# First norm's chains in turn, C's transposes in banks of their own, and four last stores instead of eight

## The chip, the core and the metric

One core of a Trainium2 chip runs the whole program. It has five engines, each with an in-order stream of instructions: TensorE (PE: matmuls and transposes, with PEld for the loading of weights), VectorE (DVE), ScalarE (ACT), GpSimd (POOL) and SyncE (SP), which here only issues DMA transfers. ScalarE issues some too. Work is handed from one to another by semaphores. The metric is the device time of one execution in microseconds (us), the median over several runs.

## What is computed

Two layers on x (256 tokens, width 1024), each of the form h + Mixer(RMSNorm(h)): first native sparse attention (16 heads in 4 groups: compressed, selected and window branches), then an S5 diagonal state-space mixer, and a final RMSNorm. The parts that the change touches:

```python
def _rmsnorm(x, g):
    y = x * lax.rsqrt(jnp.mean(x * x, axis=-1, keepdims=True) + EPS) * g

# attention: q, k, v, gates, z = split(h @ w_in); compressed, selected, window; @ w_out

# S5, parameters only (no token enters here):
    dt = jnp.exp(log_dt)[:, None]
    lre = jnp.minimum(lambda_re, -1e-4)
    mag = jnp.exp(lre * dt)
    ab_re, ab_im = mag * jnp.cos(lim * dt), mag * jnp.sin(lim * dt)
    den = lre * lre + lim * lim
    coef = (ab - 1) / lambda                     # complex
    bb_re = coef_re[..., None] * b_re - coef_im[..., None] * b_im
    bb_im = coef_re[..., None] * b_im + coef_im[..., None] * b_re
# S5, tokens: a linear scan with ab, y = Re(C x) + d * u, gelu, glu, * silu(z), @ w_out

    return _rmsnorm(h, final_norm)
```

## The kernel before

The 256 tokens lie as two tiles (NQ = 2, index j) of 128 partitions. The **first norm** sums the squares of each tile (ScalarE, L336), makes 1/sqrt with a few tiny VectorE operations (`rsqrt_steps`, tiles rs_v, rs_i, rs_t, rs_y), spreads the result along a row with a diagonal matrix and a matmul (`row_bcast`, L312 and L313; the row is copied to rrow), and multiplies the transposed x by it and by the weight: eight products xn of 128x256 (L350), one for each 128 channels. Its VectorE, GpSimd and ScalarE instructions stand in the order of the code (`manual_schedule`). Elsewhere a scheduler fixes, when the program is built, the order of each engine's instructions; on the chip each engine keeps that order.

Then the **first layer's projections** run on TensorE, each 16 matmuls of 128x256 (32 in the trace, where one fp32 matmul is two records): v0, v1 (L280), k0, k1 (L267), the gates gt, and more. Each k projection is followed by ScalarE's kh (its rounded copy, L791) and VectorE's kl (the rest, L795), which empties its PSUM bank. The small transpose cm (L875) turns a tile `rows` of parameters, which SyncE loads (L355 to L362).

Beside these projections, a generator `s5_gen` prepares the **second layer's parameters**. `chain_gen` computes dt and the powers' first factors on VectorE; their rows `nat` are transposed on TensorE into bank bg (L493), and VectorE copies them to pT (L494, all parameters with one column for each state). VectorE builds the powers pw from pT, real part pw[:, 0] and imaginary part pw[:, 1], doubling their number three times (L377, tile c is scratch), and copies eight of them to a tile named h in the trace (L532). GpSimd forms B's products from them (b1c, h, ep: six products of 128x1024, L383). C's rows are transposed in two rounds of four (q = 0, 1; L544), and ScalarE copies each round out of PSUM as c1c and c2c (L546, L548). GpSimd multiplies c1c by the real powers (ep<-c1c,pw, L383). The first four of these need the first round only, but the fourth overwrites a place from which the second round reads.

A bank of PSUM is one of eight. `bg_bank` gives the one bank of the generator, `bank(tag, 1)` one of a phase; tu and ob are tags that the attention's units use later.

At the **end**, the last projection's second tile (j = 1) is taken in three pieces (0:512, 512:768, 768:1024 columns), each added to h, squared and summed; the root follows, and `finish(1)` scales the columns and stores them. The stores are 32 rows each.

Of the kernel before, what the change touches and what calls it, by code (L numbers as in the profile page):

```python
# [8 lines left out]
F32 = mybir.dt.float32  # L9
# [3 lines left out]
ALU = mybir.AluOpType  # L13
# [33 lines left out]
def kernel(  # L47
# [52 lines left out]
    def bank(tag="b1", bufs=None):  # L100
        return phase["pool"].tile([P, 512], F32, tag=tag, name=tag, bufs=bufs or phase["bufs"])
# [181 lines left out]
    def rsqrt_steps(ss, out_, part=None):  # L283


        v = smp.tile([P, 1], F32, tag="rs_v", name="rs_v")
        V.tensor_scalar(v, ss, 1.0 / D, EPS if part is None else part, op0=ALU.mult, op1=ALU.add)
        yield
        yi = smp.tile([P, 1], I32, tag="rs_i", name="rs_i")
        V.tensor_scalar(yi, v.bitcast(I32), -0.5, float(0x5F3759DF), op0=ALU.mult, op1=ALU.add)  # L290
        yield
        y, c = yi.bitcast(F32), 1.0
        t = smp.tile([P, 1], F32, tag="rs_t", name="rs_t")
        z = smp.tile([P, 1], F32, tag="rs_y", name="rs_y")
# [31 lines left out]
    xn = actp.tile([P, KT, S], F32, tag="actT", name="xn")
    sqs = xn.rearrange("p (j k) s -> p j (k s)", j=NQ)
    bts = [bank().rearrange("p (k s) -> p k s", k=2) for _ in range(KT // 2)]
    rb, gb0 = bank(), bank()
    rrow = const.tile([P, S], F32, name="rrow")  # L330
    E_ = mybir.EngineType
    with tc.manual_schedule(engines={E_.DVE, E_.Pool, E_.Activation}):
        sums, ys = [], [[], []]
        for j in range(NQ):
            sums.append(smp.tile([P, 1], F32, tag="ss", name="ss"))
            A.activation(sqs[:, j], xin[:, j], AF.Square, accum_out=sums[j])  # L336
            for k in range(KT):
                T.transpose(bts[k // 2][:, k % 2, j * P:(j + 1) * P], xin[:, j, k * P:(k + 1) * P], ident)
        rq = [rsqrt_steps(sums[j], ys[j]) for j in range(NQ)]
        for _ in range(6):  # L340
            next(rq[0])
        for r in (rq[1], rq[0]) * 12:
            next(r, None)
        for j in range(NQ):
            row_bcast(*ys[j], rb[:, j * P:(j + 1) * P], sqs[:, j, 0:P])
        T.transpose(gb0[:, :KT], nrow, ident[:KT, :KT])
        V.tensor_copy(g0c, gb0[:, :KT])
        V.tensor_copy(rrow, rb[:, :S])
        for k in range(KT):
            V.scalar_tensor_tensor(xn[:, k], bts[k // 2][:, k % 2], g0c[:, k:k + 1], rrow,  # L350
                                   op0=ALU.mult, op1=ALU.mult)
        s5_loads()

    rows = const.tile([56, P], F32, name="rows")
    nc.sync.dma_start(rows[8:24], pe_k.rearrange("(k l) d -> k (l d)", l=2))  # L355
    nc.sync.dma_start(rows[24:40], pe_v.rearrange("(k l) d -> k (l d)", l=2))
    nc.sync.dma_start(rows[0:8], n1.rearrange("(k p) -> k p", p=P))
    nc.sync.dma_start(rows[40:48], d_skip.rearrange("(k g) c -> k (g c)", k=8))
    d4 = d_skip.rearrange("(k j u) c -> u k j c", k=8, j=4)
    r4 = rows[48:56].rearrange("k (j u c) -> k u j c", j=4, u=2)  # L360
    for u in range(2):
        nc.sync.dma_start(r4[:, u], d4[1 - u])  # L362
    colsT = const.tile([P, 56], F32, name="colsT")


    bbT.insert(0, (0, actp.tile([P, NB0, P], F32, tag="actT", name="bbT0")))
# [27 lines left out]
    def chain_gen():  # L394
# [84 lines left out]
        A.activation(nat2[:, 4:7, 1], nat[:, 4:7], AF.Copy)  # L479
        yield  # L480

    sh_ld = {}

    def s5_gen():
# [54 lines left out]
        yield  # L539

        for q in range(2):
            bt2 = bg_bank()
            for t in range(4):
                T.transpose(bt2[:, t * P:(t + 1) * P], cnat[:, 4 * q + t].rearrange("p r q -> p (r q)"), ident)  # L544
            gs = slice(32 * q, 32 * q + 32)
            A.activation(c1c[:, gs].rearrange("p g c -> p (g c)"), bt2, AF.Copy, scale=nsg)  # L546
            for hf in range(2):
                A.activation(c2c[64 * hf:64 * hf + 64, gs].rearrange("p g c -> p (g c)"),  # L548
                             bt2[64 - 64 * hf:128 - 64 * hf], AF.Copy, scale=-1.0)
            yield  # L550
# [89 lines left out]
            yield  # L640

    with tc.high_priority(-CHOFF):
        for _ in chain_gen():
            pass
    bg = s5_gen()

# [17 lines left out]
    PL.iota(cdist, pattern=[[P, NQ], [-16, NB]], base=0, channel_multiplier=1,  # L664
            allow_small_or_imprecise_dtypes=True)
    PL.tensor_scalar(cdist, cdist, -15.5, None, op0=ALU.add)
    cbias = atp.tile([P, NQ, 16, NB], F32, name="cbias")
    slopes = atp.tile([P, 16], F32, name="slopes")
    for h in range(16):
        PL.memset(slopes[:, h:h + 1], -_slope(h))  # L670
# [777 lines left out]
    def piece(i, src):  # L1448

        j, c0, c1 = pieces[i]  # L1450
        V.tensor_tensor(h1s[j][:, c0:c1], src, h1s[j][:, c0:c1], op=ALU.add)
        A.activation(ho[j][:, c0:c1], h1s[j][:, c0:c1], AF.Square, accum_out=sq[:, i:i + 1])
        if i == 4:
            return
        PL.tensor_tensor(hg[j][:, c0:c1], h1s[j][:, c0:c1], gf[:, c0:c1], op=ALU.mult)

    def finish(j, i):
        y, c = rsqrt_mean(sq[:, i:i + 1], vp[j])
        assert c == RSQRT_C
        if j == 0:  # L1460
            A.activation(ho[0], hg[0], AF.Copy, scale=y)
            for l_ in range(4):
                nc.sync.dma_start(o3[0, l_], ho[0][32 * l_:32 * l_ + 32])
            return
        A.activation(ho[1][:, 0:512], hg[1][:, 0:512], AF.Copy, scale=y)
        V.scalar_tensor_tensor(ho[1][:, 768:D], h1s[1][:, 768:D], y, gf[:, 768:D], op0=ALU.mult, op1=ALU.mult)
        V.tensor_scalar(ho[1][:, 512:768], hg[1][:, 512:768], y, None, op0=ALU.mult)
        for l_ in range(4):
            nc.sync.dma_start(o3[1, l_, :, 0:512], ho[1][32 * l_:32 * l_ + 32, 0:512])
        for l_ in range(4):  # L1470
            (nc.scalar, nc.sync)[l_ % 2].dma_start(o3[1, l_, :, 512:D], ho[1][32 * l_:32 * l_ + 32, 512:D])
# [68 lines left out]
```

## Time and profile before

| | |
|---|---|
| median of three runs | 413.06 us (411.81 to 414.19) |
| the profiled execution | 414.05 us |
| its span, first to last instruction | 412.3 us |
| busy: PE, PEld | 354.2 us (86%), 293.0 us (71%) |
| busy: DVE, ACT, POOL | 227.9 us (55%), 178.4 us (43%), 269.3 us (65%) |
| DMA | 52.03 MB, mean 126 GB/s |
| mean granted clock of TensorE | 0.933 |

A row of the timeline gives the start, the length, the engine, the line of the code, the operation, its output and input tiles, how many instructions are grouped (x4), and in square brackets how long the engine was idle before it and what ended that.

### The profile page before, as it was taken

The page shows a single profiled execution, that of the slowest core. Times are in us where ns is not written, and L with a number is a line of the kernel's source. Part 1 is how long each engine was busy: PE and PEld are TensorE (multiplying, and loading weights), DVE is VectorE, ACT ScalarE, POOL GpSimd, SP SyncE. Part 2 cuts the span into 40 slices and gives each one's busy share as a digit, 9 for nine tenths or more (in the row PEclk, how much of TensorE's full clock was granted, in tenths as well). Part 3 has the DMA queues.
Part 4 walks back from the last instruction along what each step waited for, and adds up shares of the span by engine and source line. Part 5 has one row for each costly group of instructions (what it writes and reads, how often), then busy time and mean ns, then how long its engine had stood idle before and what let it go on. Part 6 is the DMA issues. An engine that isn't in the chain of part 4 may idle for free.

```text
span 412.3 us, 6834 instructions
## 1 busy us (share of the span) xinstructions
PE 354.2 (86%) x2505; PEld 293.0 (71%) x2505; DVE 227.9 (55%) x582; ACT 178.4 (43%) x397; POOL 269.3 (65%) x281
## 2 busy tenths in 40 slices
PE   3899599999999998968998879994858599999990
PEld 3688468865888787644766657783847599999890
DVE  4969904433355243524555498563999944264243
ACT  3212420145366467566784454342513335444432
POOL 7009459989987789999544489321872476665760
PEclk9699979999999999985999999998696899999996
DMA  8964315558633315411311335996741215655403
GB/s 256 158 172 114 110 53 153 152 190 244 181 103 99 106 57 178 126 52 51 103 36 58 113 103 99 172 87 180 251 156 54 71 34 158 199 163 200 152 2 102
DMA packets 59970, 52.03 MB, mean 126 GB/s; under 512 B 21928, under 2 KB 52704, under 8 KB 59872
## 3 DMA queue, kind: packets, MB, share of 16 engines
q1 hardware_dynamic: 49536, 50.41, 43.9%
q10 hardware_dynamic: 10400, 1.18, 2.2%
q8 instruction: 20, 0.33, 0.4%
q14 instruction: 14, 0.11, 0.1%
HBM read 48.17 MB, written 1.05 MB: 119 GB/s over the span
## 4 chain that ended last, share of the span: by engine, by line
PE 57%; DVE 16%; SPq 6%; POOL 6%; DMA 5%; issue 5%; ACT 3%; DVEq 0%; ACTq 0%; POOLq 0%
PE b L267 16%; SPq L1181 5%; PE b L280 4%; PE b L224 4%; PE b L225 4%; PE b L226 4%; PE ob L986 3%; PE tu L973 2%; PE b L246 2%; PE b L244 2%; PE b L245 2%; DVE pw L377 2%; POOL wl L209 2%; PE cm L745 2%; DVE bbT L1357 2%
## 5 line engine op out<-in xcount | busy, mean ns | idle before, releaser
L209 POOL TENSOR_TENSOR wl<-raw,wh 128x1024 fp32r<-128x1024 f32 x30 | 74.3, 2480 | 48.3 <-ACT wh L207 48.1
L267 PE MATMUL b<-xn,raw 128*128 128x256 f32 (+1 forms) x400 | 94.9, 390 | 4.7 <-DVE kl L795 3.4
L267 PEld LDWEIGHTS b<-xn,raw 128*128 128x128 f32 (+1 forms) x400 | 74.1, 190 | 18.6 <-issue 4.6
L207 ACT ACTIVATE wh<-raw 128x1024 fp32r<-128x1024 f32 x48 | 50.8, 1058 | 67.0 <-PE b L225 20.7
L209 DVE TENSOR_TENSOR wl<-raw,wh 128x1024 fp32r<-128x1024 f32 x18 | 26.3, 1462 | 26.3 <-ACT wh L207 26.3
L959 ACT ACTIVATE pt<-pt,nm 128x128 f32<-128x128 f32 (+1 forms) x64 | 28.3, 444 | 24.8 <-DVE nm L955 24.7
L225 PE MATMUL b<-yl,wh 128*128 128x256 f32 x128 | 36.1, 283 | 0.0
L224 PE MATMUL b<-yh,wh 128*128 128x256 f32 x128 | 36.1, 284 | 0.0
L226 PE MATMUL b<-yh,wl 128*128 128x256 f32 x128 | 36.0, 283 | 0.0
L975 DVE COPY pT<-tu 128x512 f32<-128x512 f32 x24 | 16.6, 691 | 25.4 <-PE tu L973 24.7
L968 ACT ACTIVATE pt<-pt,su 128x128 f32<-128x128 f32 (+1 forms) x64 | 24.6, 443 | 11.6 <-DVE su L966 11.5
L224 PE MATMUL b<-xp,wh 128*128 128x256 f32 x64 | 20.2, 317 | 5.7 <-ACT wh L207 5.7
L224 PEld LDWEIGHTS b<-yh,wh 128*128 128x128 f32 x128 | 24.5, 192 | 0.2 <-issue 0.2
L225 PEld LDWEIGHTS b<-yl,wh 128*128 128x128 f32 x128 | 24.6, 192 | 0.0
L226 PEld LDWEIGHTS b<-yh,wl 128*128 128x128 f32 x128 | 24.5, 192 | 0.0
L383 POOL TENSOR_TENSOR ep<-c1c,pw 128x1024 f32<-128x1024 f32 x8 | 16.0, 2022 | 10.3 <-ACT c1c L546 5.3
L955 DVE CUSTOM_DVE_ANT_0 pt<-su,b 128x128 f32<-128x128 f32 (+1 forms) x64 | 19.4, 351 | 4.7 <-PE su L943 4.7
L226 PE MATMUL b<-xp,wl 128*128 128x256 f32 x64 | 20.1, 316 | 1.6 <-POOL wl L209 1.6
L383 POOL TENSOR_TENSOR bbn<-bbn,bbt 128x512 f32<-128x512 f32 x16 | 20.4, 1274 | 0.6
L383 POOL TENSOR_TENSOR bbn<-b1c,h 128x512 f32<-128x512 f32 x16 | 17.8, 1111 | 4.6 <-PE bg L604 4.4
L986 PE MATMUL ob<-pT,vsw 128*64 128x128 f32 x192 | 17.4, 297 | 3.4 <-DVE pT L975 3.4
L225 PE MATMUL b<-xp,wh 128*128 128x256 f32 x64 | 19.8, 311 | 0.0
(319 smaller groups left out, 874.1 us busy)
## 6 DMA issues: line engine op xcount, KB each, us to landing
raw<-in_l_w_in_dram SPq DMA_DIRECT2D x44, 512.0 KB, 4.0
raw<-in_l_w_out_dram SPq DMA_DIRECT2D x16, 512.0 KB, 3.9
raw<-in_l_w_glu_dram SPq DMA_DIRECT2D x16, 512.0 KB, 3.6
raw<-in_l_cmp_k_w_dram SPq DMA_DIRECT2D x4, 512.0 KB, 3.9
raw<-in_l_cmp_v_w_dram SPq DMA_DIRECT2D x4, 512.0 KB, 3.9
xin<-in_x_dram SPq DMA_DIRECT2D x2, 512.0 KB
h<-in_x_dram SPq DMA_DIRECT2D x8, 128.0 KB, 3.3
tm<-kt__2197 SPq DMA_DIRECT2D x4, 128.0 KB
```

What stands on the lines that cost most here:

```text
L207: A.activation(hi, raw, AF.Copy)
L209: lo_eng[-1].tensor_tensor(lo, raw, hi.bitcast(F32), op=ALU.subtract)
L224: T.matmul(dst, a, xh[:, k], start=(k == 0 and e == 0), stop=False)
L225: T.matmul(dst, a, xl[:, k], start=False, stop=False)
L226: T.matmul(dst, b, xh[:, k], start=False, stop=(k == KT - 1 and e == len(dsts) - 1))
L267: T.matmul(dst, w[:, i, e * m:(e + 1) * m], xn[:, k], start=(k == 0 and e == 0), stop=(k == KT - 1 and e == len(dsts) - 1))
L383: PL.tensor_tensor(o, a, b_, op=op)
L955: V.tensor_tensor_reduce(o.rearrange("p t k -> p (t k)"), sb[:, i * w + br * nk:i * w + (br + 1) * nk], self.b8[hf][:, S - nk:S], -0.125, ...
L959: A.activation(o, o, AF.Exp, scale=-1.0, bias=self.nm[:, j, hf, br:br + 1], accum_out=self.su[:, j, hf, br:br + 1])
L968: A.activation(o, o, AF.Copy, scale=r)
L986: T.matmul(self.ob[64 * hf:64 * hf + 64, j * P:(j + 1) * P], vsw[:, kt, br, 64 * g:64 * g + 64], p_, start=first, stop=last, tile_position ...
L1181: nc.sync.dma_start(tm[16 * s_:16 * s_ + 16, 16 * j:16 * j + 16].rearrange("p q l c -> p q (l c)")[:, :, 16 * l_:P], kt_[32 * j:32 * j + 1 ...
```

## The change

The first norm's second sum of squares goes from ScalarE to VectorE, and the two chains of tiny operations run strictly in turn. The diagonals are written into the tile cbias, so that tile is opened earlier. The first three pieces of `chain_gen` are issued behind the norm's products, no longer among them. C's two rounds of transposes take the banks tu and ob instead of bg. At the end, GpSimd no longer multiplies the piece 512:768, one VectorE operation covers 512:1024, and tile j = 1 is stored by four transfers of 32x1024, one from SyncE and three from ScalarE, instead of eight of 32x512.

```diff
+    att = tc.tile_pool(name="att", bufs=1, reuse_waits="tile")
+    atp = att.__enter__()
+    cbias = atp.tile([P, NQ, 16, NB], F32, name="cbias")
...
     with tc.manual_schedule(engines={E_.DVE, E_.Pool, E_.Activation}):
-        sums, ys = [], [[], []]
-        for j in range(NQ):
-            sums.append(smp.tile([P, 1], F32, tag="ss", name="ss"))
-            A.activation(sqs[:, j], xin[:, j], AF.Square, accum_out=sums[j])
+        sums, ys = smp.tile([P, NQ], F32, name="ss0"), [[], []]
+        A.activation(sqs[:, 0], xin[:, 0], AF.Square, accum_out=sums[:, 0:1])
+        V.tensor_tensor_reduce(sqs[:, 1], xin[:, 1], xin[:, 1], 1.0, 0.0, ALU.mult, ALU.add, sums[:, 1:2])
+        for j in range(NQ):
             for k in range(KT):
                 T.transpose(bts[k // 2][:, k % 2, j * P:(j + 1) * P], xin[:, j, k * P:(k + 1) * P], ident)
-        rq = [rsqrt_steps(sums[j], ys[j]) for j in range(NQ)]
-        for _ in range(6):
-            next(rq[0])
-        for r in (rq[1], rq[0]) * 12:
+        rq = [rsqrt_steps(sums[:, j:j + 1], ys[j]) for j in range(NQ)]
+        T.transpose(gb0[:, :KT], nrow, ident[:KT, :KT])
+        for r in rq * 12:
             next(r, None)
         for j in range(NQ):
-            row_bcast(*ys[j], rb[:, j * P:(j + 1) * P], sqs[:, j, 0:P])
-        T.transpose(gb0[:, :KT], nrow, ident[:KT, :KT])
+            row_bcast(*ys[j], rb[:, j * P:(j + 1) * P], cbias[:, j, 0:8].rearrange("p h n -> p (h n)"))
...
         s5_loads()
+        chain = chain_gen()
+        for _ in range(3):
+            next(chain)
...
         for q in range(2):
-            bt2 = bg_bank()
+            bt2 = bank(("tu", "ob")[q], 1)
             for t in range(4):
                 T.transpose(bt2[:, t * P:(t + 1) * P], cnat[:, 4 * q + t].rearrange("p r q -> p (r q)"), ident)
...
     with tc.high_priority(-CHOFF):
-        for _ in chain_gen():
+        for _ in chain:
             pass
...
-        if i == 4:
+        if i >= 3:
             return
...
-        V.scalar_tensor_tensor(ho[1][:, 768:D], h1s[1][:, 768:D], y, gf[:, 768:D], op0=ALU.mult, op1=ALU.mult)
-        V.tensor_scalar(ho[1][:, 512:768], hg[1][:, 512:768], y, None, op0=ALU.mult)
+        V.scalar_tensor_tensor(ho[1][:, 512:D], h1s[1][:, 512:D], y, gf[:, 512:D], op0=ALU.mult, op1=ALU.mult)
         for l_ in range(4):
-            nc.sync.dma_start(o3[1, l_, :, 0:512], ho[1][32 * l_:32 * l_ + 32, 0:512])
-        for l_ in range(4):
-            (nc.scalar, nc.sync)[l_ % 2].dma_start(o3[1, l_, :, 512:D], ho[1][32 * l_:32 * l_ + 32, 512:D])
+            (nc.sync if l_ == 1 else nc.scalar).dma_start(o3[1, l_], ho[1][32 * l_:32 * l_ + 32])
```

What stands on TensorE from cm to the gates before (one row of 128x256 x16 is one projection: v1 and k0, k1 by their b tiles; gt is the one of 48x256; nat are the powers' rows, ep C's rows):

```order
L875 MATMUL cm<-ident,rows 128x56
L280 MATMUL b_402<-raw,xn 128x256 x14
L493 MATMUL bg<-ident,nat_106 128x64 x4
L280 MATMUL b_402<-raw,xn 128x256 x2
L267 MATMUL b_433<-xn,raw 128x256 x9
L493 MATMUL bg<-ident,nat_106 128x64 x3
L267 MATMUL b_433<-xn,raw 128x256 x7
L267 MATMUL b_485<-xn,raw 128x256 x16
L544 MATMUL bg<-ident,ep 128x128 x4
L267 MATMUL b_530<-xn,raw 48x256 x8
L267 MATMUL b_558<-xn,raw 128x256 x4
L544 MATMUL bg<-ident,ep 128x128 x4
```

And after the change, the same place on TensorE (v1 is b_401, k0 b_432, k1 b_484, gt b_529):

```order
L878 MATMUL cm<-ident,rows 128x56
L285 MATMUL b_401<-raw,xn 128x256 x16
L272 MATMUL b_432<-xn,raw 128x256 x4
L499 MATMUL bg<-ident,nat_106 128x64 x4
L272 MATMUL b_432<-xn,raw 128x256 x11
L499 MATMUL bg<-ident,nat_106 128x64 x3
L272 MATMUL b_432<-xn,raw 128x256
L272 MATMUL b_484<-xn,raw 128x256 x16
L550 MATMUL tu<-ident,ep 128x128 x4
L550 MATMUL ob<-ident,ep 128x128
L272 MATMUL b_529<-xn,raw 48x256 x8
L550 MATMUL ob<-ident,ep 128x128 x3
```

The powers' first transposes moved behind the last two matmuls of v1 and the first four of k0, the second ones behind fifteen of k0 instead of nine. C's first round stands where it stood, in bank tu; one transpose of the second round moved ahead of the gates and the other three right behind them.

On SyncE, the stores at the end of the program before (tm is the tile of the results):

```order
L1463 DMA out_dram<-tm 32x1024 x4
L1469 DMA out_dram<-tm 32x512 x4
L1471 DMA out_dram<-tm 32x512 x2
```

After, on SyncE, the same stores:

```order
L1466 DMA out_dram<-tm 32x1024 x4
L1471 DMA out_dram<-tm 32x1024
```

And on ScalarE after, whose last row read 32x512 x2 before:

```order
L1464 ACTIVATE tm<-tm,rs_y 128x1024
L1468 ACTIVATE tm<-tm,rs_y 128x512
L1471 DMA out_dram<-tm 32x1024 x3
```

Of the second tile's eight stores four are left; three of the four moved behind ScalarE's product of the columns 0:512, and SyncE issues one.

## Rows read from the trace of the kernel before

**Rows 1.** Chain that ended last on the page: share of the span by engine.

```profile
PE 57%; DVE 16%; SPq 6%; POOL 6%; DMA 5%; issue 5%; ACT 3%; DVEq 0%; ACTq 0%; POOLq 0%
```

**Rows 2.** Stretches: length, busy us of PE, PEld, DVE, ACT, POOL; PE clock, DMA share, GB/s.

```profile
46.40:56.40 10.00, 6.48 (x18) 3.31 (x19) 5.68 (x20) 3.23 (x6) 5.97 (x3) 0.66 0.19 52
...
80.00:150.00 70.00, 68.99 (x428) 54.07 (x428) 28.32 (x103) 34.21 (x108) 59.09 (x62) 1.00 0.50 145
150.00:198.00 48.00, 41.49 (x251) 30.49 (x250) 18.31 (x68) 31.63 (x87) 46.30 (x56) 0.86 0.32 104
```

**Rows 3.** TensorE's timeline: start us, us, line, operation, tiles, idle time before and its releaser.

```profile
13.11 10.00 PE L280 MATMUL b<-raw,xn 128*128 128x256 f32 x32 [1.81 <-issue]
23.05 0.27 PE L875 MATMUL cm<-ident,rows 56*128 56x56 f32 x1
23.24 6.31 PE L280 MATMUL b<-raw,xn 128*128 128x256 f32 x28
29.48 0.46 PE L493 MATMUL bg<-ident,nat 64*128 64x64 f32 x4
...
46.49 0.66 PE L544 MATMUL bg<-ident,ep 128*128 128x128 f32 x4 [1.16 <-DVE pT L494]
50.58 8.45 PE L267 MATMUL b<-xn,raw 128*48 128x256 f32 x24 [3.43 <-DVE kl L795]
```

**Rows 4.** VectorE's timeline, 30 to 52 us.

```profile
30.61 1.93 DVE L372 TENSOR_SCALAR cis<-pT,sgn 128x64 f32<-128x64 f32 x1
...
36.49 2.37 DVE L532 COPY h<-pw 128x128 f32<-128x128 f32 x1
...
41.11 2.26 DVE L377 TENSOR_TENSOR pw<-pw,c 128x64 f32<-128x64 f32 x1
...
46.35 0.42 DVE L377 TENSOR_TENSOR pw<-pw,c 128x256 f32<-128x256 f32 x1
...
48.05 0.63 DVE L532 COPY h<-pw 128x128 f32<-128x128 f32 x4
48.60 3.48 DVE L795 TENSOR_TENSOR kl<-b,kh 64x256 fp32r<-64x256 f32 x8
```

**Rows 5.** GpSimd's timeline, 30 to 55 us.

```profile
30.48 2.00 POOL L383 TENSOR_TENSOR b1c<-ep,pT 128x1024 f32<-128x1024 f32 x1 [22.10 <-DVE pT L494]
...
40.88 2.42 POOL L383 TENSOR_TENSOR h<-h,ep 128x1024 f32<-128x1024 f32 x1
48.62 5.97 POOL L383 TENSOR_TENSOR ep<-c1c,pw 128x1024 f32<-128x1024 f32 x3 [5.33 <-ACT c1c L546]
```

**Rows 6.** ScalarE's timeline, first norm and C.

```profile
5.75 1.06 ACT L336 ACTIVATE xn<-xin 128x1024 f32<-128x1024 f32 x1 [0.31 <-DMA xin<-in_x_dram]
...
47.80 0.69 ACT L546 ACTIVATE c1c<-bg,nsg 128x512 f32<-128x512 f32 x1
```

**Rows 7.** VectorE's timeline, first norm.

```profile
7.94 0.14 DVE L287 TENSOR_SCALAR rs_v<-ss 128x1 f32<-128x1 f32 x1
...
9.62 0.16 DVE L299 SCALAR_TENSOR_TENSOR rs_y<-rs_t,rs_y 128x1 f32<-128x1 f32 x1
...
11.68 0.53 DVE L419 RECIPROCAL den<-den 64x64 f32<-64x64 f32 x1
...
12.15 3.21 DVE L350 SCALAR_TENSOR_TENSOR xn<-b,g0c,rrow 128x256 f32<-128x256 f32 x8
```

**Rows 8.** SyncE's queue, the last loads of the rows.

```profile
18.41 1.56 SPq L362 DMA_DIRECT2D rows<-in_l_d_dram  x2
```

**Rows 9.** SyncE's queue, last stores.

```profile
409.15 0.84 SPq L1471 DMA_DIRECT2D out_dram<-tm  x2
```

**Rows 10.** ScalarE's queue, last stores.

```profile
406.29 0.85 ACTq L1471 DMA_DIRECT2D out_dram<-tm  x2
```

**Rows 11.** VectorE's timeline, last product.

```profile
405.50 0.48 DVE L1466 SCALAR_TENSOR_TENSOR tm<-h,rs_y,gf 128x256 f32<-128x256 f32 x1
```

**Rows 12.** TensorE's timeline, the taps of the second layer.

```profile
241.56 1.08 PE L634 MATMUL bg<-ep,b1c 128*32 128x128 f32 x32 [2.56 <-ACT kt__2197 L638]
```

More of the change, by code (lines that the diff above doesn't have):

```diff
@@ L324 @@
         prefetch(w_in0, 4 * c_, 4, FIRST[1], 256)
[L326 to L332, printed above, removed]
-        sums, ys = [], [[], []]
-        for j in range(NQ):
-            sums.append(smp.tile([P, 1], F32, tag="ss", name="ss"))
-            A.activation(sqs[:, j], xin[:, j], AF.Square, accum_out=sums[j])
-            for k in range(KT):
-                T.transpose(bts[k // 2][:, k % 2, j * P:(j + 1) * P], xin[:, j, k * P:(k + 1) * P], ident)
-        rq = [rsqrt_steps(sums[j], ys[j]) for j in range(NQ)]
-        for _ in range(6):
-            next(rq[0])
-        for r in (rq[1], rq[0]) * 12:
-            next(r, None)
-        for j in range(NQ):
-            row_bcast(*ys[j], rb[:, j * P:(j + 1) * P], sqs[:, j, 0:P])
-        T.transpose(gb0[:, :KT], nrow, ident[:KT, :KT])
[L347 to L366, printed above, removed]
     MAGIC = 12582912.0
@@ L480, in chain_gen @@
         yield
+    xn = actp.tile([P, KT, S], F32, tag="actT", name="xn")
+    sqs = xn.rearrange("p (j k) s -> p j (k s)", j=NQ)
+    bts = [bank().rearrange("p (k s) -> p k s", k=2) for _ in range(KT // 2)]
+    rb, gb0 = bank(), bank()
+    rrow = const.tile([P, S], F32, name="rrow")
+    E_ = mybir.EngineType
+    with tc.manual_schedule(engines={E_.DVE, E_.Pool, E_.Activation}):
+        sums, ys = smp.tile([P, NQ], F32, name="ss0"), [[], []]
+        A.activation(sqs[:, 0], xin[:, 0], AF.Square, accum_out=sums[:, 0:1])
+        V.tensor_tensor_reduce(sqs[:, 1], xin[:, 1], xin[:, 1], 1.0, 0.0, ALU.mult, ALU.add, sums[:, 1:2])
+        for j in range(NQ):
+            for k in range(KT):
+                T.transpose(bts[k // 2][:, k % 2, j * P:(j + 1) * P], xin[:, j, k * P:(k + 1) * P], ident)
+        rq = [rsqrt_steps(sums[:, j:j + 1], ys[j]) for j in range(NQ)]
+        T.transpose(gb0[:, :KT], nrow, ident[:KT, :KT])
+        for r in rq * 12:
+            next(r, None)
+        for j in range(NQ):
+            row_bcast(*ys[j], rb[:, j * P:(j + 1) * P], cbias[:, j, 0:8].rearrange("p h n -> p (h n)"))
+        V.tensor_copy(g0c, gb0[:, :KT])
+        V.tensor_copy(rrow, rb[:, :S])
+        for k in range(KT):
+            V.scalar_tensor_tensor(xn[:, k], bts[k // 2][:, k % 2], g0c[:, k:k + 1], rrow,
+                                   op0=ALU.mult, op1=ALU.mult)
+        s5_loads()
+        chain = chain_gen()
+        for _ in range(3):
+            next(chain)
+    rows = const.tile([56, P], F32, name="rows")
+    nc.sync.dma_start(rows[8:24], pe_k.rearrange("(k l) d -> k (l d)", l=2))
+    nc.sync.dma_start(rows[24:40], pe_v.rearrange("(k l) d -> k (l d)", l=2))
+    nc.sync.dma_start(rows[0:8], n1.rearrange("(k p) -> k p", p=P))
+    nc.sync.dma_start(rows[40:48], d_skip.rearrange("(k g) c -> k (g c)", k=8))
+    d4 = d_skip.rearrange("(k j u) c -> u k j c", k=8, j=4)
+    r4 = rows[48:56].rearrange("k (j u c) -> k u j c", j=4, u=2)
+    for u in range(2):
+        nc.sync.dma_start(r4[:, u], d4[1 - u])
+    colsT = const.tile([P, 56], F32, name="colsT")
+    bbT.insert(0, (0, actp.tile([P, NB0, P], F32, tag="actT", name="bbT0")))
     sh_ld = {}
@@ L650, in adv @@
                 next(bg, None)
-    att = tc.tile_pool(name="att", bufs=1, reuse_waits="tile")
-    atp = att.__enter__()
     dist = atp.tile([P, S], F32, name="dist")
@@ L666 @@
     PL.tensor_scalar(cdist, cdist, -15.5, None, op0=ALU.add)
-    cbias = atp.tile([P, NQ, 16, NB], F32, name="cbias")
     slopes = atp.tile([P, 16], F32, name="slopes")
```

## The prediction

> **What bounds the kernel now.** I read the chain of work that ended last first. TensorE holds 57% of it, VectorE 16%, SyncE's queue and GpSimd 6% each [rows 1]. An average over stages says little, so the span was cut into stretches next [rows 2]. From 80 to 150 us TensorE is busy 68.99 of 70 us, so whatever it is late by at 80 it is still late by at 150. From 150 to 198 GpSimd is busy 46.30 of 48 and TensorE 41.49: there GpSimd sets the pace. But GpSimd had 11 us of idle time in the 70 us ahead, so it reaches 150 waiting for TensorE's results and not ahead of them. I therefore count a delay of TensorE around 60 us as one of the end, and look for slack only between 150 and 198.
>
> The stretch from 46.4 to 56.4 us is the one place near the change where TensorE stands: 6.48 of 10 us busy at a mean granted clock of 0.66 [rows 2]. TensorE's own timeline shows why [rows 3]: C's transposes wait 1.16 us for VectorE's copy pT, and the 24 matmuls of gt start at 50.58 after 3.43 us of waiting for VectorE's kl. Behind kl on VectorE, read backwards [rows 4], stand four copies h (48.05), the last products of the powers pw, and ahead of them ten operations between 30.61 and 43.37. Those of them that wait take 1.9 to 2.4 us. GpSimd's timeline tells what for [rows 5]: six products of 128x1024 run from 30.48 to 43.30, and VectorE's last of the ten, 41.11 + 2.26 = 43.37, ends with GpSimd's last, 40.88 + 2.42 = 43.30. A copy h of 128x128 took 2.37 us there and 0.63 / 4 = 0.16 us at 48.05, when GpSimd was idle [rows 4]. So a VectorE operation from SBUF to SBUF waits out GpSimd's product, and ten of them pass in six products. kl, which reads PSUM, does not: its eight take 3.48 / 8 = 0.44 us each beside GpSimd's three ep products [rows 4, 5].
>
> In the Trainium skill, "SBUF — State Buffer", section "Who interferes with whom", VectorE and GpSimd share a pair of ports that whoever starts first holds for the whole instruction, against VectorE operations with two SBUF inputs or in a two-port mode, and a VectorE instruction with one SBUF input outside these modes does not contend. The 2.37 us of the copy agree with the first part. By the second part, if the four h copies were in no such mode, they would run free, kl would come at the lower bound below, +3.6, and the sum would be 3.6 + 0.35 - 1.9 = +2.05: 415.1.
>
> **The first norm.** Before, the second chain of small operations runs from 7.94 to 9.78, the first product xn starts at 12.15, and the first matmul at 13.11, 0.96 us later [rows 7, 3]. Now VectorE squares row j=1 itself as soon as it has arrived; ScalarE's second Square started at 5.75 on that arrival [rows 6]. The operation does not occur before; a 128x1024 Square of ScalarE takes 1.06 [rows 6], and one xn product of 128x256 takes 3.21 / 8 = 0.40 [rows 7], so 1.06 to 1.6 us for it; I take 1.2. Both chains then start near 7.1. Eight steps of two chains in turn, at some 0.23 us a step (ten operations in 9.78 - 7.94 = 1.84 us, each pair of neighbours with one wait), end near 8.9. The two diagonals, two small matmuls and the copies to the row take what they took, 12.15 - 9.78 = 2.37 us, less the lambda chain's operations that stood between them and now follow xn. Of these the reciprocal alone is 0.53 [rows 7]; with the smaller ones I take 0.9, which leaves 1.5 us. The first matmul is at 8.9 + 1.5 + 0.96 = 11.35, 1.75 earlier. GpSimd's two bias passes, which now run behind the small matmuls, lie beside xn, which reads PSUM.
>
> **What is given back at once.** The small transpose cm at 23.05 needs the rows that SyncE loads last, at 18.41 and 1.56 us long [rows 3, 8]. ScalarE now issues B and C's loads after one Square instead of two (its second was 1.06 us long and ended 1.4 us behind the first), and SyncE's row loads wait for b_re and c_re to land. So they land about 1.4 us sooner at best. cm then stands at 21.5, between 20.5 (the whole gain and a little) and 22.3 (half of it).
>
> **The first transposes of the powers.** They stand at 29.48, 6.43 us after cm [rows 3]. The order moves them behind six more matmuls (two of v1, four of k0, twelve halves in the trace). 28 halves took 6.31 us [rows 3], so this is 12 x 0.225 = 2.7 us. They stand 9.1 us after cm: 30.6, 1.1 us later than before, though TensorE is 1.55 us ahead. The gain of the norm would have to reach 20.35 for cm before this comes out at nothing. VectorE's powers and GpSimd's six products follow these transposes, and shift by +1.1: the last real power, 46.35 + 0.42 = 46.77, to 47.9 [rows 4].
>
> **C's transposes.** Their 1.16 us of waiting goes, since they no longer share bg. ScalarE's c1c stood right behind its kh, which follows TensorE; both move with TensorE by 1.55, and c1c is ready near 47.0 instead of 47.80 + 0.69 = 48.49 [rows 6]. GpSimd's first ep product started at 48.62, when c1c came and when VectorE had just finished its last h copy (48.68) [rows 5, 4]. Now c1c is there before the last real power, so ep starts at 48.0, and VectorE still has eight SBUF operations ahead of kl: two pair, one c, one pw, four h, in 48.60 - 46.77 = 1.8 us if free. This relation does not hang on cm: both times move with it. Three ep products stand there, 5.97 us [rows 5]; the fourth waits for transposes behind gt.
>
> At ten in six products, eight operations outlast the three products: free at 48.0 + 5.97 + 0.2 = 54.2, so kl is 5.6 us later than 48.60. If the two pair operations and the c slip through ahead of the first product, two products hold the rest: 52.2, +3.6. If none is held, +1.1. gt's start, 1.98 us behind kl's [rows 3, 4], moves with it. I take the middle of 3.6 and 5.6, +4.6. The first transposes and the lock together turn TensorE's lead into a lag. TensorE then starts gt at the lower of its two levels, as before (24 halves in 8.45 us, 0.35 each against 0.225, at a stretch mean of 0.66 [rows 2, 3]), so the lag neither grows nor shrinks there.
>
> **Later.** TensorE waits 2.56 us for ScalarE's kt before 241.56 [rows 12]. VectorE's two tiny operations for a root now stand ahead of the addition that kt waits for: 0.15 to 0.4 us, I take +0.35. Exchanges of neighbours from 184 to 230: nothing, within 0.7 both ways.
>
> **The last stores.** Before, SyncE issues its last two stores from 409.15, 0.84 long, until 409.99, ScalarE two from 406.29, and the span ends at 412.3 [rows 9, 10]. Now one scalar_tensor_tensor of 128x512 replaces the 128x256 one (405.50, 0.48 [rows 11]) and a multiply: 0.7 to 0.96 us, over at 406.4. Then ScalarE issues three stores of 0.43 each (0.85 / 2), until 407.7, and SyncE its one. That is 2.3 us sooner. Each is twice as large, which may add some tenths to its landing: -1.9, between -1.3 and -2.4.
>
> **Sum.** +4.6 + 0.35 - 1.9 = +3.05 us. On the profiled execution of 414.05 (span 412.3 and 1.75 around it) that is 417.1. The median of the runs is 413.06, 0.99 less, so the forecast is 416.1, rounded to 416.0.
>
> **Rivals.**
> One, not slower: GpSimd's ep does not hold VectorE (the copies and products run free, or ep starts behind them). For it: the lock was seen with other operands for six of the eight operations. Against: a copy h itself was held. Then the front costs +1.1, and the sum is 1.1 + 0.35 - 1.9 = -0.45: 412.6; with cm at 20.5 and the stores at -2.4, 411.0. It decides whether kl begins before 50.5. Chance 0.20.
> Two, no change: one product alone holds VectorE, +1.1 + 2.0, or GpSimd's pace from 150 to 198 swallows two or three us of the lag, since TensorE idles 6.5 us there [rows 2]. Sum about +0.5: 413.6. Against the second: GpSimd's ep work is late too. Chance 0.22.
> Three, the norm does not give what it says: the rows land no sooner, cm stays at 22.3 to 23, the first transposes shift by 1.9 to 2.6, and the sum is 3.9 to 4.6: 417 to 417.7. For it: SyncE's row loads wait for b_re and c_re, which were slow before. Chance 0.13.
> The forecast itself has 0.45, with a range of its own from 414.9 (+3.6, stores -2.1) to 417.5 (+5.6, stores -1.5).
>
> **Range and chances.** About 0.5% (2.07 us) is what a measurement of this kernel can tell from no change. The range reaches from 411.0, the good end of rival one, to 418.0, the far end of three. Faster by over 0.5% (under 411.0) takes the good part of rival one and a swallowed lag: 0.13. Within: most of rivals one and two and the lowest of the forecast: 0.32. Slower: 0.55.
>
> **What would show it.** Right: the first matmul near 11.4, cm near 21.5, the first nat transposes near 30.6, C's transposes without a wait near 45, ep at 48.0, h copies of about 2 us each where they were 0.16, kl at 52 to 54.5, gt at 54 to 56.5, the last issue over near 407.7 less the shift. Wrong: kl before 50.5, or gt within 1 us of 50.58; a gap in 150 to 198 that shrinks by the lag; cm beyond 22.5; or stores that land as late as before.

## The result, and the profile after

The changed kernel takes 422.36 us (median of six executions, 421.06 to 426.94), the kernel before 413.00 in the same comparison: a ratio of 1.0236, 95% interval 1.0207 to 1.0265, or +9.4 us between the medians. In a later comparison, c0 below, the ratio of the same kernel was 1.0159 (1.0117 to 1.0202); the two intervals do not overlap, and why is not known. The ratios leave out executions over 1.5% slower than the fastest of their kernel: two of c1's four, the profiled one among them, and one of e1's ten. The profiled execution is the slowest of the six, 426.94 with a span of 425.1; c0's profile has a span of 421.0, and where the two differ both numbers are given.

The page of the changed kernel: span, busy time, and the chain that ended last.

```profile
span 425.1 us, 6829 instructions
...
PE 359.4 (85%) x2505; PEld 297.1 (70%) x2505; DVE 230.9 (54%) x583; ACT 177.0 (42%) x395; POOL 267.2 (63%) x280
...
PE 61%; DVE 17%; DMA 6%; POOL 6%; issue 5%; ACT 3%; SPq 0%; ACTq 0%; DVEq 0%; POOLq 0%
```

No engine has much more to do than before. The time has to be looked for in waits and, as will be seen, in TensorE's clock. TensorE's timeline of the changed kernel, to be read beside [rows 3]:

```profile
11.64 9.87 PE L285 MATMUL b<-raw,xn 128*128 128x256 f32 x32 [1.63 <-DVE xn L467]
...
23.26 0.24 PE L878 MATMUL cm<-ident,rows 56*128 56x56 f32 x1 [1.76 <-DMA rows<-in_l_d_dram]
23.43 8.86 PE L285 MATMUL b<-raw,xn 128*128 128x256 f32 x32
...
33.95 0.46 PE L499 MATMUL bg<-ident,nat 64*128 64x64 f32 x4
...
47.05 0.60 PE L550 MATMUL tu<-ident,ep 128*128 128x128 f32 x4
...
60.18 2.34 PE L272 MATMUL b<-xn,raw 128*48 128x256 f32 x5 [12.42 <-DVE kl L798]
```

The first matmul is 1.47 us earlier, as was meant. At cm the lead is gone: cm waits for the rows (1.76). The powers' first transposes stand at 33.95 instead of 29.48, and gt waits 12.42 us for kl instead of 3.43 and starts 9.6 us later. VectorE ahead of kl, to be read beside [rows 4]:

```profile
50.84 0.42 DVE L339 TENSOR_TENSOR pw<-pw,c 128x256 f32<-128x256 f32 x1
51.17 0.42 DVE L334 TENSOR_SCALAR pair<-pT 64x96 f32<-64x96 f32 x2
51.62 2.13 DVE L339 TENSOR_TENSOR c<-pw 128x256 f32<-128x256 f32 x1
53.79 2.13 DVE L339 TENSOR_TENSOR pw<-pw,c 128x256 f32<-128x256 f32 x1
55.95 2.34 DVE L538 COPY h<-pw 128x128 f32<-128x128 f32 x4
58.21 3.48 DVE L798 TENSOR_TENSOR kl<-b,kh 64x256 fp32r<-64x256 f32 x8
```

GpSimd and ScalarE in the same place:

```profile
51.43 6.37 POOL L345 TENSOR_TENSOR ep<-c1c,pw 128x1024 f32<-128x1024 f32 x3 [3.65 <-DVE pw L339]
```

```profile
49.68 0.69 ACT L552 ACTIVATE c1c<-tu,nsg 128x512 f32<-128x512 f32 x1
```

c1c is over at 50.37, the last real power at 51.26, and GpSimd starts ep at 51.43 with VectorE's eight operations still to come. c and pw take 2.13 us each, where 0.43 and 0.42 are their free length, and each ends 0.3 us or less behind the end of a product of GpSimd. kl starts 6.78 us behind ep's start. In the second profile all of this is the same but 2.9 us earlier: ep at 48.54, kl at 55.32, gt at 57.30.

Behind that the lag (how much later a matmul starts or ends than the same one before) goes to 8.9 us at 94 and stays within a microsecond of it to 200. Then the first profile shows what the prediction did not look for: TensorE in the re-ordered end of the attention, and the granted clock there.

```profile
220.88 0.50 PE L945 MATMUL su<-kh,qs 128*128 128x512 f32 x1 [0.34 <-DVE nm L958]
...
222.81 0.84 PE L976 MATMUL tu<-ident,pt 128*128 128x128 f32 x4 [1.19 <-ACT pt L971]
...
224.43 1.10 PE L989 MATMUL ob<-pT,vsw 128*64 128x128 f32 x14 [0.78 <-DVE pT L978]
```

```profile
226.00:232.00 6.00, 5.84 (x29) 4.28 (x28) 2.29 (x8) 3.38 (x11) 1.58 (x6) 0.77 0.06 19
...
250.00:256.00 6.00, 3.12 (x46) 2.24 (x39) 5.79 (x21) 3.46 (x8) 5.69 (x16) 0.72 0.39 128
256.00:262.00 6.00, 6.00 (x51) 4.58 (x49) 3.77 (x10) 1.79 (x3) 5.76 (x10) 0.71 0.09 33
```

Three waits of TensorE stand within four microseconds, and the clock falls to 1.2 GHz for a part of the stretch behind them. It falls again at the end of the wait for kt, which is 2.88 us long instead of 2.56 [rows 12]. Whether these waits are the cause is taken up below: c2 has the first three, and d1 the last, without the fall. Before, the clock was 1.00 from 198 to 262. The lag goes from 8.0 at the last scores (su, 221) to 11.3 at the last product of the attention (235) and to 14.5 at the last tap (263).

The last stores, beside [rows 9 to 11]:

```profile
418.91 1.76 SPq L1466 DMA_DIRECT2D out_dram<-tm  x4
420.78 0.36 SPq L1471 DMA_DIRECT2D out_dram<-tm  x1
```

```profile
419.96 1.33 ACTq L1471 DMA_DIRECT2D out_dram<-tm  x3
```

From the first tile's stores to the end of the span it is 425.1 - 418.91 = 6.2 us, before 412.3 - 405.29 = 7.0. Another 0.2 to 0.3 us lies in the root ahead of them, where an operation rs_t of VectorE took 0.69 us beside GpSimd's second multiply before and takes 0.22 now.

### The profile page after: what moved, and what is told of

It is laid out like the page before. It is cut to its first block, busy times and chain, and to the rows that moved or that the text cites. A ratio compares the mean times of both kernels' runs of the same rounds, so it can differ in the third digit from the quotient of the medians.

```text
span 425.1 us, 6829 instructions
## 1 busy us (share of the span) xinstructions
PE 359.4 (85%) x2505; PEld 297.1 (70%) x2505; DVE 230.9 (54%) x583; ACT 177.0 (42%) x395; POOL 267.2 (63%) x280
## 4 chain that ended last, share of the span: by engine, by line
PE 61%; DVE 17%; DMA 6%; POOL 6%; issue 5%; ACT 3%; SPq 0%; ACTq 0%; DVEq 0%; POOLq 0%
PE b L272 16%; PE b L231 4%; PE b L229 4%; PE b L230 4%; PE b L249 3%; PE b L250 3%; PE b L251 3%; PE ob L989 3%; PE tu L976 3%; DVE pw L339 2%; PE b L285 2%; DMA ep<-in_l_c_re_dram 2%; POOL bbn L345 2%; POOL wl L214 2%; PE cm L748 2%
## 5 line engine op out<-in xcount | busy, mean ns | idle before, releaser
L229 PE MATMUL b<-xp,wh 128*128 128x256 f32 x64 | 19.5, 307 | 4.8 <-ACT wh L212 4.8
L1413 PE MATMUL b<-ep,bbT 128*32 128x128 f32 x128 | 9.5, 341 | 13.0 <-DVE zs L1395 13.0
L285 PE MATMUL b<-raw,xn 128*128 128x256 f32 x64 | 18.7, 465 | 1.6 <-DVE xn L467 1.6
```

The lines of the kernel that those rows point to most:

```text
L229: T.matmul(dst, a, xh[:, k], start=(k == 0 and e == 0), stop=False)
L285: T.matmul(dst, xn[:, k, j * P:(j + 1) * P], w[:, i], start=(k == 0 and j == 0), stop=(k == KT - 1 and j == len(dsts) - 1))
```

## Experiments

c0 to c3 and e1 start from the changed kernel, the others from the kernel before (f1's diff is shown against the changed kernel). All ratios are to the kernel before on the same chip.

**c0, the changed kernel again.** No edit.

> The changed kernel once more, for a second profile. Theory: what it loses before the gates (gt starts at 60.18 instead of 50.58) is the same in every execution, so gt starts within 0.3 of 60.2 again and the time is 421 to 423.5; the lag that grows in the first profile from 8.0 us at 213 to 14.5 at 263 is partly a matter of TensorE's granted clock (0.77, 0.72 and 0.71 there, 1.00 before) and differs from execution to execution, so the span here is near 420.5 and the lag at the last matmul near 9 to 10. Rival: the growth from 213 to 263 belongs to the re-ordered attention, and is there again with the clock at 1.00.

Measured: 420.7 us, ratio 1.0159 (1.0117 to 1.0202). TensorE in this execution:

```profile
22.07 0.24 PE L878 MATMUL cm<-ident,rows 56*128 56x56 f32 x1 [0.76 <-DMA rows<-in_l_d_dram]
22.24 7.17 PE L285 MATMUL b<-raw,xn 128*128 128x256 f32 x32
...
31.08 0.46 PE L499 MATMUL bg<-ident,nat 64*128 64x64 f32 x4
...
57.30 5.44 PE L272 MATMUL b<-xn,raw 128*48 128x256 f32 x16 [12.41 <-DVE kl L798]
```

The expectation that gt stands at 60.2 every time is wrong. Here the rows landed 1.2 us sooner and v1 ran at 2.4 GHz (7.17 us instead of 8.86), and everything up to gt is 2.9 us earlier. The wait for kl is the same to 0.01 us. The growth is there again, from 4.2 us (last su) to 7.6 (last product of the attention) to 10.7 (last tap), with the clock again low at 222 and at 249 to 255. So it is not the chance of one execution, though with the clock low again this run cannot tell the order from the clock; c2 can.

**c1, C's transposes back in the generator's bank.**

```diff
-            bt2 = bank(("tu", "ob")[q], 1)
+            bt2 = bg_bank()
```

> The changed kernel with C's transposes back in the generator's bank; the first norm and the stores stay changed. Theory (c1c that comes before the last real power lets GpSimd's ep in ahead of VectorE's last eight operations): the first four transposes wait for pT (50.9), c1c is ready near 52.3 and ep starts there instead of 51.43; VectorE has c and pw behind it by then, and only the h copies are held by one product: kl near 54.5 instead of 58.21, gt near 56.5, time 418.5 to 419. Rival (the lateness is all of the first norm's making: rows and the powers' transposes come late): kl and gt stay at 58 and 60, time 422.

Measured: ratio 1.0111 (1.0036 to 1.0185), the median of all four 421.24. In the profiled execution kl starts at 55.63 and gt at 57.61, as in c0. My theory expected 3.7 us back from 60.18 and, against c0's 57.30, got nothing: the loss does not need the new banks. ep starts 1.0 us later than in c0, but then all four copies h are still ahead of kl, and they take 6.15 us. The ratio rests on two executions, 415.78 and 420.18, and is too wide to tell c1 from c0.

**c2, the real powers written last.** In each doubling the subtraction that ends the real part becomes the sixth operation instead of the fourth.

```diff
-            vtt(pr[:, o], pr[:, i_], br_)
-            vtt(c0[:, 0:w], pi[:, i_], bi_)
             vtt(pi[:, o], pr[:, i_], bi_)
-            vtt(pr[:, o], pr[:, o], c0[:, 0:w], ALU.subtract)
             vtt(c0[:, 0:w], pi[:, i_], br_)
+            vtt(pr[:, o], pr[:, i_], br_)
             vtt(pi[:, o], pi[:, o], c0[:, 0:w], ALU.add)
+            vtt(c0[:, 0:w], pi[:, i_], bi_)
+            vtt(pr[:, o], pr[:, o], c0[:, 0:w], ALU.subtract)
```

> The changed kernel with the order of the six operations of each doubling of the powers turned round, so that the real part, for which GpSimd's ep waits, is written last and not fourth; nothing else. Theory: ep starts near 52.5 instead of 51.43, when VectorE has only the four h copies left, and the program's order now puts the first four kl behind one of them: kl at 52.6 to 54.5, gt at 54.6 to 56.5 instead of 60.18, time 416.8 to 418.7. Rival (VectorE is slow there for another reason than GpSimd's products): c and pw, which took 2.13 each, take as long, gt stays within 1.5 us of 60, time 421 to 423.

Measured: 417.71 us, ratio 1.0102 (1.0055 to 1.0149). VectorE, with GpSimd's ep from 53.56 to 59.55 beside it:

```profile
53.43 0.23 DVE L538 COPY h<-pw 128x128 f32<-128x128 f32 x1
53.57 1.72 DVE L798 TENSOR_TENSOR kl<-b,kh 64x256 fp32r<-64x256 f32 x4
55.32 4.31 DVE L538 COPY h<-pw 128x128 f32<-128x128 f32 x3
59.66 1.73 DVE L798 TENSOR_TENSOR kl<-b,kh 64x256 fp32r<-64x256 f32 x4
```

c and pw are back at 0.42 us, the four kl beside ep run free (0.43 each), and the three copies behind them are held until ep is over. gt is at 55.55, though the rows landed late in this execution (cm at 23.95). The rival, a cause other than GpSimd's products, falls.

This profile settles something else. In the end of the attention it has the three waits of the changed kernel in the same places, and the clock stays at 1.00 (the third number from the end of the last line):

```profile
217.34 0.50 PE L945 MATMUL su<-kh,qs 128*128 128x512 f32 x1 [0.33 <-DVE nm L958]
...
219.27 0.84 PE L976 MATMUL tu<-ident,pt 128*128 128x128 f32 x4 [1.20 <-ACT pt L971]
...
220.89 1.09 PE L989 MATMUL ob<-pT,vsw 128*64 128x128 f32 x14 [0.78 <-DVE pT L978]
```

```profile
222.00:228.00 6.00, 5.68 (x33) 3.92 (x34) 2.72 (x9) 4.61 (x15) 2.46 (x6) 1.00 0.13 45
```

The lag grows by 2.0 us here, where it grows by 3.3 to 3.4 in c0 and the first profile. So the waits cost 2.0 us, and the fall of the clock, which does not follow from them every time, another 1.4.

**c3, the row loads ahead of B and C's in the program.**

```diff
+    rows = const.tile([56, P], F32, name="rows")
+    nc.sync.dma_start(rows[8:24], pe_k.rearrange("(k l) d -> k (l d)", l=2))
...
     xn = actp.tile([P, KT, S], F32, tag="actT", name="xn")
```

> The changed kernel with SyncE's six loads of the parameter rows put into the program ahead of B and C's loads, so that they don't wait for those. Theory (cm at 23.26 waits 1.76 us for the rows, TensorE's clock falls in this gap and the v1 projection takes 8.86 us instead of 7.1): cm stands right behind v0, at 21.4 to 21.6, v1 takes 7.1 to 7.3, the powers' first transposes stand at 30.5 to 31.0 instead of 33.9, and all behind them moves by 3 to 3.4: gt near 57, time near 419. Rival: the rows are not what holds cm, or the gain is lost to a later load; cm near 23, time 422.

Measured: 421.9 us, ratio 1.0204 (1.0162 to 1.0246). The edit did not move what it was to move: SyncE's row loads still wait for b_re (until 14.04) and for b_im (until 18.13; 18.30 in c0), since each signals its landing by the same semaphore as the load it waits for, and cm stands at 21.95 with 0.76 us of waiting, as in c0. What the rows cost is not told by this run. The kernel runs as c0 does, and its ratio is a third measurement of the change.

**d1, d2, d3: each part of the change alone on the kernel before.** d1 takes the first norm's part, d2 the one line of the banks, d3 the last stores; the diffs are those pieces of the change.

> The kernel before with the first norm's part of the change alone (chains in turn, its squares, the lambda chain behind xn, cbias opened earlier); C's transposes in the old bank and the stores as before. Theory now (this part alone moves the powers' first transposes behind k0 and so makes GpSimd's ep meet VectorE's copies, and it alone re-orders the attention): the whole loss and the store's gain on top, gt at 57 to 58, time 420 to 423. Rival, which the prediction held (the banks bring c1c forward and so the loss): 414 to 415.

> The kernel before with C's transposes in the banks tu and ob, nothing else. Theory: they no longer wait 1.16 us for pT, but c1c still follows ScalarE's kh, which ends at 47.77, and ep still starts near 48.6 when VectorE's copies are over; gt near 50.6, time within 1 us of 413. Rival of the prediction (the missing wait lets ep in ahead of VectorE): ep at 47, kl 3 to 5 us later, time 416 to 418.

> The kernel before with the last stores' part alone. The changed kernel's trace shows 416.2 to 425.1 from the last matmul's end to the span's end where the kernel before shows 402.37 to 412.3, so about 1.0 us is gained: 412. The prediction's -1.9 would give 411.1; a rival, that the lower lag there is chance, 413.

Measured: d1 419.74, ratio 1.017 (1.012 to 1.022); d2 413.14, 0.9977 (0.9955 to 0.9999); d3 411.34, 0.9939 (0.9923 to 0.9956). Alone, the norm's part loses 7.0 us by the ratio, the banks are worth nothing or a little, the stores gain 2.5 us. The three add up to +3.6 us, and the whole change measured +6.6 (c0) to +9.7 by the ratio: the parts do not add, and what the banks cost together with the norm's part the runs do not separate from the scatter of the executions (d1's reach from 419.32 to 425.07).

d1's expectation, gt at 57 to 58 and 420 to 423 us, missed:

```profile
21.79 0.24 PE L878 MATMUL cm<-ident,rows 56*128 56x56 f32 x1 [2.21 <-DMA rows<-in_l_d_dram]
21.96 7.17 PE L285 MATMUL b<-raw,xn 128*128 128x256 f32 x32
...
55.56 6.91 PE L272 MATMUL b<-xn,raw 128*48 128x256 f32 x24 [6.90 <-DVE kl L798]
...
247.38 1.08 PE L640 MATMUL bg<-ep,b1c 128*32 128x128 f32 x32 [2.87 <-ACT kt__2196 L644]
```

c1 and d1 are the same program up to the last stores, and c1's gt came at 57.61. The copies h began 0.23 us ahead of ep in d1 and 0.02 us ahead of it in c1; two of the four were held in d1, each for one product, and three in c1. A fifth of a microsecond there made nearly two at gt. cm waits 2.21 us here, longer than in the first profile, and v1 keeps its clock; the taps wait 2.87 us for kt, and the clock stays at 1.00 from 246 to 255.

In d1 ScalarE's kh is long over when C's transposes come, and c1c waits only for them. GpSimd and VectorE of d1:

```profile
49.59 5.97 POOL L345 TENSOR_TENSOR ep<-c1c,pw 128x1024 f32<-128x1024 f32 x3 [4.99 <-ACT c1c L552]
```

```profile
49.36 4.30 DVE L538 COPY h<-pw 128x128 f32<-128x128 f32 x4
53.58 3.48 DVE L798 TENSOR_TENSOR kl<-b,kh 64x256 fp32r<-64x256 f32 x8
```

In d2 the transposes no longer wait for pT, but c1c still stands behind kh, and ep starts when the copies are all but over. ScalarE, GpSimd and VectorE of d2:

```profile
47.14 0.69 ACT L546 ACTIVATE c1c<-tu,nsg 128x512 f32<-128x512 f32 x1
```

```profile
47.96 5.98 POOL L383 TENSOR_TENSOR ep<-c1c,pw 128x1024 f32<-128x1024 f32 x3 [5.33 <-ACT c1c L546]
```

```profile
47.38 0.63 DVE L532 COPY h<-pw 128x128 f32<-128x128 f32 x4
47.93 3.48 DVE L795 TENSOR_TENSOR kl<-b,kh 64x256 fp32r<-64x256 f32 x8
```

So in the kernel before it is a matter of some 0.3 us that the copies are through before ep: ep at 49.59 in d1 holds them for 4.30 us, ep at 47.96 in d2 lets them pass.

**e1, kl ahead of the copies.** The changed kernel with c2's edit, and the copies behind a tiny write that depends on c1c.

```diff
-        for s_, l_ in enumerate(SLOT_L):
-            V.tensor_copy(pws[:, :, s_], pw[:, :, 8 - l_])
...
+        A.activation(pws[0:1, 0, :, 0:1], c1c[0:1, 0:8, 0:1], AF.Copy)
+        for s_, l_ in enumerate(SLOT_L):
+            V.tensor_copy(pws[:, :, s_], pw[:, :, 8 - l_])
```

> The changed kernel with the real powers written last (as in the run with the order turned round) and, besides, the eight copies h put behind a one-row write that ScalarE makes after c1c, so that the order on VectorE has all eight kl ahead of the copies: nothing that GpSimd's ep could hold stands ahead of kl. Theory: kl at 49 to 52.5 according to cm, 1.9 us behind the real powers at most, gt 2 us behind it at 51 to 54.5, instead of 57.3 to 60.2; time 414 to 416.5, above the kernel before by the rows' lateness, the moved transposes and two stretches of lower clock after 220 us. Rival (other work holds gt): gt at 55 or later, time 418 or more.

Measured: 415.74 us, ratio 1.0045 (1.0017 to 1.0072). VectorE and TensorE of e1:

```profile
49.51 3.48 DVE L799 TENSOR_TENSOR kl<-b,kh 64x256 fp32r<-64x256 f32 x8
53.02 3.10 DVE L557 COPY h<-pw 128x128 f32<-128x128 f32 x4
```

```profile
51.48 5.36 PE L272 MATMUL b<-xn,raw 128*48 128x256 f32 x16 [6.47 <-DVE kl L799]
```

gt is back within 0.9 us of before, and about 5 us of c0's loss with it. At 97 us this kernel is 0.5 us ahead of the kernel before, at 226 it is 2.1 behind: the end of the attention, with its waits and a fall of the clock.

**f1 to f3, the norm in an order that leaves the rest alone.** f1 is the kernel before with the norm's part without VectorE's square and without the lambda chain in the block. f2 adds the banks, the stores and e1's edits. f3 has f2's additions on the old norm.

```diff
-        V.tensor_tensor_reduce(sqs[:, 1], xin[:, 1], xin[:, 1], 1.0, 0.0, ALU.mult, ALU.add, sums[:, 1:2])
+        A.activation(sqs[:, 1], xin[:, 1], AF.Square, accum_out=sums[:, 1:2])
...
         chain = chain_gen()
-        for _ in range(3):
-            next(chain)
```

> The kernel before with the half of the first norm's part that leaves the rest of the program's order alone: the two chains strictly in turn and the diagonals in cbias, but both squares on ScalarE and the lambda chain not issued in the norm's block. All instructions of all engines behind the norm stand as before, the powers' first transposes and the attention too. Theory (the loss is made by the order that follows from the norm's part, not by the norm on the chip): first matmul near 12.0 instead of 13.11, cm bound by the rows at 22 to 23, ep behind the last copy h as before, no lower clock at 222 and 250, time 412 to 413.5. Rival (the earlier start, the diagonals in cbias or the loads lose the time): 416 or more.

> The same with the banks tu and ob, the last stores of the change, the real powers written last, and the eight copies h behind kl. Theory: kl right behind the powers, gt at 48.5 to 49.5, 1 to 2 us ahead of before, and the stores' 2.3 us: 409 to 410.5. Rival (TensorE's lead is lost where GpSimd sets the pace from 150 to 198): 411 to 412.

> The kernel before with its own first norm, and the banks tu and ob, the last stores, the real powers last and the copies h behind kl. Theory: as the run with the norm in order, less what that norm brings (0 to 1 us): 409.5 to 411. If the norm in order brings nothing, the two are equal.

Measured: f1 413.4, ratio 0.9997 (0.9975 to 1.0019); f2 410.42, 0.9927 (0.9901 to 0.9954); f3 410.07, 0.9925 (0.9897 to 0.9953). With the old order behind it this half of the norm's part costs nothing, and it gains nothing either: f2 and f3 are equal. But the first matmul of f1 came at 13.15 and not at 12.0, so no run has the earlier first matmul with the old order; and which of the two pieces that f1 leaves out, VectorE's square or the lambda chain behind xn, moves the order was not tried. TensorE of f1:

```profile
28.34 0.46 PE L497 MATMUL bg<-ident,nat 64*128 64x64 f32 x4
...
49.43 7.85 PE L272 MATMUL b<-xn,raw 128*48 128x256 f32 x24 [3.43 <-DVE kl L796]
```

f2 and e1 have the front alike at 97 us (1.1 and 0.5 us ahead of before), and differ in the attention's order. Their stretch 214 to 220, e1 first and f2 second:

```profile
214.00:220.00 6.00, 5.21 (x27) 3.98 (x28) 2.15 (x9) 3.48 (x11) 1.53 (x5) 0.72 0.27 89
```

```profile
214.00:220.00 6.00, 5.22 (x30) 3.52 (x30) 2.82 (x9) 3.89 (x14) 1.93 (x6) 1.00 0.26 89
```

f2 is 1.0 us ahead of before at the attention's last product, e1 2.1 behind it. In all five kernels with the old order (d2, d3, f1 to f3) the lag at that product is the one at the last scores, within 0.03 us. f2 and f3 beat the kernel before by 3 us, of which the stores alone give 2.5, and the changed one by more than that.

## Why the prediction was wrong, step by step

The side was right, and so was the mechanism of the loss at the front. The size was not: +3.05 us forecast, +9.4 measured, outside the range. The two profiles, +12.8 and +8.6 us by their spans, lie on either side of that.

| step | forecast | measured (first profile; c0) |
|---|---|---|
| first matmul | 11.35 | 11.64; 11.8 |
| cm | 21.5 (20.5 to 22.3) | 23.26; 22.07 |
| powers' first transposes | 30.6 | 33.95; 31.08 |
| ep starts | 48.0 | 51.43; 48.54 |
| kl starts | 52.2 to 54.2 | 58.21; 55.32 |
| gt, against 50.58 | +3.6 to +5.6, taken +4.6 | +9.6; +6.7 |
| 184 to 230 | 0 (0.7 both ways) | +3.3; +3.4 |
| taps at 241 | +0.35 | +3.2; +3.1 |
| given back elsewhere | 0 | -2.2; -3.4 |
| last stores | -1.9 | -1.1; -1.2 in the traces, -2.5 by d3's ratio |
| sum, from gt on | +3.05 | +12.8; +8.6 |

Two terms of the sum failed. The larger is the end of the attention and the taps, 6.5 us in both profiles where the sum has 0 and +0.35. The other is gt: +4.6 forecast, 5.0 us more in the first profile and 2.1 more in c0.

**At the front the step that failed is "I take the middle of 3.6 and 5.6, +4.6".** The lower bound let the two pair operations and c slip through ahead of the first product. Only the pair operations did; c was held at once, and kl came 6.78 us behind ep's start in both profiles, where the forecast had 4.2 to 6.2. The upper bound was nearly right; the three products took 6.37 us instead of 5.97. Of the 5.0 us by which gt missed in the first profile 1.6 are this and 3.4 are ep's late start, which came from cm and v1; of c0's 2.1 they are 1.6 and 0.5. From the last real power to kl it is 58.21 - 51.26 = 6.95 us, before 48.60 - 46.77 = 1.83: 5.1 us of holding, where +4.6 less +1.1 left 3.5 for it. c2 and e1 show that this is GpSimd's doing: with kl ahead of what is held, gt is back at 51.48. The copies were held as well, so the case of 415.1, in which they run free, falls.

**"cm then stands at 21.5"** took the whole of ScalarE's 1.4 us for the rows, and named b_re and c_re as what they wait for. They waited for b_im too, which took 13.4 us to land in c0, and TensorE waited for them, 1.76 and 0.76 us in the two profiles. In the first profile TensorE's clock fell in v1 as well, the 1.7 us between 8.86 and 7.17. The length of the wait does not explain it: with waits of 1.90 (c1), 2.21 (d1) and 2.59 us (e1) v1 took 7.17, with 2.48 (c2) 8.74. What decides stays open. Rival three had this delay, without the clock.

**"Exchanges of neighbours from 184 to 230: nothing" put a term at nothing that measured +3.3.** I priced instructions that change places, not waits of TensorE that come to stand close together. In all six profiles of kernels with the whole norm part and gt late by 5 to 9.6 us, the lag grew in the attention's end by 2.0 to 3.4 us, and by 3.4 in e1, whose gt is hardly late. It grew in none of the five with the old order, so it belongs to the order. The waits are 2.0 us of it, as c2 shows with its clock at 1.00; the rest, 1.4, is the clock.

**"+0.35" for the taps was right for the wait and left out the clock.** The wait for kt grew by 0.3 us, and in d1 and e1, where the clock stayed, the lag grew by just that. In the first profile, c0, c1 and c3 the clock fell at the end of the wait and cost 2.8 us more, in c2 1.5. The longer wait cannot be the cause by itself, since d1 and e1 have the same 2.87 us. The clock fell there in the kernels whose gt was 5.0 us late or more, d1 excepted; why stays open.

**"Their 1.16 us of waiting goes" gave the banks a part that the loss does not need.** d2 shows no loss with the banks alone, d1 and c1 a loss without them. What matters is the order of two times: c1c stood behind kh, and so behind TensorE; VectorE's copies stand behind the powers' transposes. The norm's part moves the transposes 2.7 us back against TensorE, as the step on them said, and in d1 that alone makes ep meet the copies. The step itself was right: cm to transposes is 9.0 us in c0, for 9.1 forecast.

**The stores** gained 1.1 us in the trace, not 1.9. The last issue was over 2.6 us earlier, counted from the last matmul, but from there to the end of the span it took 425.1 - 421.29 = 3.8 us instead of 412.3 - 409.99 = 2.3: the "tenths" for landing were 1.5 us. Whether their double size or their close start makes that, no run tells apart. d3's ratio gives 2.5 us (1.8 to 3.2). Its profile shows 0.9 of it behind the first stores and 0.2 to 0.3 ahead of them; where the rest comes from the runs don't show.

The bound of 80 to 150 us held: the lag of c0 was 5.5 us from 86 to 176. That GpSimd's pace from 150 to 198 might swallow some was rival two; the lag was 4.2 at the last scores (217), so 1.3 us was. Another 1.2 went in gt, where the forecast had the lag stay, and 0.9 behind the taps. Rival two's own sum was off: one product held gives 1.1 + 2.0 + 0.35 - 1.9 = +1.55, 414.6, not +0.5.

## What to carry to other kernels

A small gain at the start can move work of a scheduler's choice far behind it: before an edit is priced, list every engine's order for the whole program, and price each moved wait by who stands behind it. Where many short VectorE operations meet a string of long GpSimd products, write down which comes first, by how much, and put what TensorE waits for ahead of both. A margin of 0.3 us that nobody wrote down is the first thing an edit somewhere else will use up. Where waits of TensorE move, give the clock a term of its own, with a chance: here the same waits came with the fall in some executions and without it in others.

## What the runs showed of the hardware

Short VectorE operations from SBUF to SBUF that meet a string of GpSimd's 128x1024 products are let through at one or two for each product (ten in six products before): the held ones took 1.8 to 2.4 us each. Beside three products of 2.0 to 2.2 us three of eight were held in the changed kernel (6.8 us in all), three of four in c1 (6.15), two of four in d1 (4.30), two of three in c2 (4.31). A copy takes 0.16 us when GpSimd is idle. VectorE's kl, which reads PSUM, ran at 0.43 us each beside the same products in c2. The clock of TensorE fell behind waits of 0.34, 1.19 and 0.79 us between 217 and 221 in c0; the same work with waits of 0.78, 0.23 and 0.78 us between 211 and 218 in f2 kept it, but c2, with 0.33, 1.20 and 0.78 us in four microseconds, kept it too.
